# Weight preparation in a streaming trunk: how far ahead weights are begun, where their low parts are added, and what the order planner charges

## The chip, the cores and the metric

The kernel runs on one core of one Trainium2 chip. The metric is device microseconds of one execution. One execution was also taken with the hardware profiler; its records are what the views of the trace show.

## The reference, cut to what matters

One layer of a hybrid encoder is applied to 512 prompt rows and 64 sample rows of width 1024, which the kernel treats as one block of 576 columns, features on the 128 partitions:

```
x += Mixer(RMSNorm(x))         # gated DeltaNet branch and GLA branch, both in chunks, sigmoid-gated merge, output projection
x += CrossAttn(RMSNorm(x))     # 4 heads into 256 memory tokens (keys and values projected here too)
x += ConvFFN(RMSNorm(x))       # up-projection to 2*2816, causal conv of width 3, silu(gate)*value, down-projection
y  = RMSNorm(x)
```

Outputs are y for both groups of rows, the new matrix states and convolution states, and the projected memory keys and values. All data are float32, so the projections need more than one pass of reduced precision.

## The kernel before, in words

**Weights and their two parts.** Every weight tile is 128 x 1024 float32. A DMA from SyncE's queue loads it from HBM into a raw tile (`raw_tile`, ring of RAWB = 3). It is then split into a high part h (the value rounded to the matmul's format) and a low part lo (what the rounding lost), each a tile of a ring of WB = 6 (`w_tile`). Activations are split likewise. A projection of one weight (`proj`) is, for each of eight blocks k of 128 rows, h*a, h*b and lo*a, each in two column groups of 256 and 320: 48 matmuls. With `late=True` the sixteen lo*a matmuls come after all the others. The first two weights are split by hand at the start; `emit_weight` does all the others.

**Two ways to make lo.** For most weights ScalarE casts raw into h, and then VectorE or GpSimd, whichever the planner expects to be done first (`X`), computes raw - h into lo. For the kinds in `SUMMED` (before: only the FFN's "up" and "dn") `split_summed` lets ScalarE write -raw, rounded, into lo, and raw, rounded, into h; then a DMA issued by GpSimd adds raw to lo, so that the remainder is left. Before, that DMA reads the raw tile in SBUF.

**How far ahead.** `weight(kind, idx)` hands the next weight of the fixed list WORDER to TensorE's code and calls `fetch`, which emits weights until the room of five (or two) tiles is used: the current weight and one more. A part of the FFN's down-projection is done by a product scheme (`emit_product`, `products`): for each pair of output tiles seven products P1, Q5, Q6, P2, P3, Q7, Q4 in place of eight, with weights that are sums of quarters, computed by VectorE into slots named ws. A product's weight takes one w tile (h and lo in its halves), a pair holds two raw tiles until its last product has been split.

**Order of the work.** All queues are in order, and the program is written out by a planner in Python, the class `Driver`. Main code (`main`) yields matmuls of the projections; side chains (`c_gdn`, `c_gla`, `c_att`, `c_gate`, `c_act`) are generators that the driver advances between main pieces. For each instruction the driver charges a cost (FIXED and PACE for VectorE V, ScalarE A, GpSimd G and DMA D; `matmul` for TensorE), works out when its operands would be there, and puts it into a heap by that time; a step of a chain is placed on TensorE once its inputs are expected to be ready. So the costs decide the order of every queue, and an expectation that is too early shows as TensorE waiting.

**Memory.** A pool `tp` holds the small tiles of the side chains (about 24 KB per partition); it stays open to the end. A slot ring of 57 tiles holds everything of 576 columns; PSUM has two double-bank tiles (`big`) and four single-bank ones (`sm`).

**Stages on the time axis.** Start to 30 us; head projections with the DeltaNet and GLA chains between them, to about 360 us; the rest of the gate projections, `out` and `wo` to 540; memory keys and values, queries and attention to 690 (the `mo` projection reaches to about 720); the FFN from there, in which stretches of `up` projections alternate with the product scheme (about 810 to 855, 925 to 970, 1035 to 1085, 1130 to 1150); the final norm and stores. Nearly all instructions are recorded under L211, the line at which the driver issues them, so tiles and times tell them apart.

Of the kernel before, what the change touches and what calls it, by code (L numbers as in the profile page):

```python
# [17 lines left out]
P = 128  # L18
# [11 lines left out]
WB = 6  # L30
NGDN = 2
# [89 lines left out]
SUMMED = ("up", "dn")  # L121
# [11 lines left out]
class Engine:  # L133
# [8 lines left out]
    def weigh(self, calls):  # L142
        cost, aps, outs = 0.0, [], []
        for name, args, kw in calls:
            a = [v for v in list(args) + list(kw.values()) if hasattr(v, "tensor")]
            if kw.get("op") == ALU.pow:
# [3 lines left out]
            cost += 0.05 * (name == "activation") + 0.06 * (name == "scalar_tensor_tensor" or self.key == "V" and a[0].shape[-1] <= 128 and any(v.space == bass.MemoryType.PSUM for v in a[1:]))  # L150
            cost += 0.09 * (kw.get("accum_out") is not None or hasattr(kw.get("scale"), "tensor"))
# [4 lines left out]
        return cost, outs, aps  # L156

    def when(self, calls):
        cost, outs, aps = self.weigh(calls)
        return self.drv.place(self.key, self.drv.open(outs, aps), cost, False) + cost  # L160

    def together(self, calls, extra=0.0):

        cost, outs, aps = self.weigh(calls)
        self.drv.note(self.key, cost + extra, outs, aps, [(getattr(self.eng, name), args, kw) for name, args, kw in calls])
# [15 lines left out]
class Driver:  # L181
# [4 lines left out]
    FIXED = dict(V=0.07, A=0.05, G=0.12, D=0.01)  # L186
    PACE = dict(V=1 / 960, A=1 / 1140, G=1 / 470, D=512 / 360e3)

    def __init__(self, pe, sync):
        self.pe, self.sync = pe, sync  # L190
        self.chains = []
        self.done = set()
        self.now = 0.0
        self.half = None
        self.last = 0.0
        self.wrote = {}
        self.seen = {}
        self.ringed = {}
        self.busy = dict(V=[], A=[], G=[], D=[])
        self.ring = {}  # L200
        self.heap = []
        self.count = 0
# [48 lines left out]
    def free_at(self, tag):  # L251
        return min((max([0.0] + list(self.wrote.get(old, {}).values()) + list(self.seen.get(old, {}).values())), old)
                   for old in self.ring[tag])
# [4 lines left out]
    def place(self, key, t, cost, keep=True):  # L258

        q = self.busy[key]  # L260
        t = max(t, self.now - BACK)
        i = 0
        while i < len(q) and q[i][0] < t + cost:
            t = max(t, q[i][1])
            i += 1
        if keep:
            q.insert(i, (t, t + cost))
        if len(q) > 200:
            del q[:100]
        return t  # L270

    def note(self, key, cost, outs, aps, fns):
        start = self.place(key, self.open(outs, aps), cost)
        end = start + cost
        self.mark(self.wrote, end, outs)
        self.mark(self.seen, end, aps)
        self.last = max(self.last, end)
        self.put(start, fns)

    def load(self, out, in_):  # L280
        cost = self.FIXED["D"] + free(out) * self.PACE["D"]
        start = self.place("D", max(self.ready_at(out), self.latest(self.seen, out)) + 1.6, cost)
        self.mark(self.wrote, start + cost, [out])
        self.put(start - 1.6, [(self.sync.dma_start, (out, in_), {})])

    def store(self, out, in_):
        cost = self.FIXED["D"] + free(in_) * self.PACE["D"]
        start = self.place("D", self.ready_at(in_) + 1.6, cost)
        self.mark(self.seen, start + cost, [in_])
        self.put(start - 1.6, [(self.sync.dma_start, (out, in_), {})])  # L290
# [21 lines left out]
    def matmul(self, out, lhsT, rhs, **kw):  # L312
        n, m = free(rhs), lhsT.shape[-1]
        if lhsT.dtype == F32:
            cost = max(n / 2400, 0.053) if m == 32 else max(n * 4 / 2400 + 0.005, 0.213 if m > 64 else 0.11)
# [75 lines left out]
def tile_trunk(ctx, tc, xT, memT, wt, wd, vec, cst, w0, wgate, st_gdn, st_conv, st_gla, st_ffn, ckT, cv,  # L391
# [12 lines left out]
    tp = ctx.enter_context(tc.tile_pool(name="tp", bufs=6))  # L404
    pb = ctx.enter_context(tc.tile_pool(name="pb", bufs=2, space=bass.MemoryType.PSUM))
    pq = ctx.enter_context(tc.tile_pool(name="pq", bufs=4, space=bass.MemoryType.PSUM))
    cnt = [0]

# [28 lines left out]

    def raw_tile():
        return drv.rotate("raw", RAWB, wp.tile([P, 1024], F32, tag="raw", name=nm("wr"), bufs=RAWB))

    def w_tile():
        return drv.rotate("w", WB, wp.tile([P, 1024], F32R, tag="w", name=nm("w"), bufs=WB))

    def emit_weight(i):
# [6 lines left out]
        if kind == "dn":  # L451
            m, p = idx
            n = len(PARTS[p]) * 128
            DMA(raw[:, :n], wd[m, :, PART0[p] * 128:PART0[p] * 128 + n])
        else:
            DMA(raw, wt[WIDX[(kind, idx)]])
        h, lo = w_tile(), w_tile()
        if kind in SUMMED:
            split_summed(h[:, :n], lo[:, :n], raw[:, :n])
# [3 lines left out]
        wready[i] = (h, lo)  # L463
# [8 lines left out]
    def emit_product(pair, prod):  # L472
# [3 lines left out]
        if prod == "P1":  # L476
            r = halves_of[pair] = []
            for i in range(2):
                raw = raw_tile()
                DMA(raw[:, :2 * n], wd[m + i, :, PART0[p] * 128:PART0[p] * 128 + 2 * n])  # L480
                r += [raw[:, 0:n], raw[:, n:2 * n]]
        r = halves_of[pair]
        a11, a12, a21, a22 = r[:4]
# [11 lines left out]
        if prod in ("P1", "P2", "Q4"):  # L495
            split_summed(h, lo, src)
        else:
            A.copy(h, src)
            X.tensor_tensor(lo, src, f(h), op=ALU.subtract)
        return h, lo  # L500

    def weight(kind, idx, ahead=1):
# [29 lines left out]
    for t_ in raws:  # L532
        drv.rotate("raw", RAWB, t_)
# [75 lines left out]
    def tile_proj(kind, idx, xs, box):  # L609
# [3 lines left out]
        yield from proj(ps, wh, wl, xs, late=kind in SUMMED and idx > 0)  # L613
# [238 lines left out]
    def c_gdn(h):  # L852
# [178 lines left out]
        for i in range(4):  # L1031
# [3 lines left out]
            pc = sm()  # L1035
            if S is not None:
                PE.matmul(pc[0:n, 0:128], ks_[i], S, start=True, stop=True)
# [3 lines left out]
            else:  # L1041
                R = vb[:, i, :]
            PE.matmul(pc[0:n, 128:256], Y[:, i, :], R, start=True, stop=True)
# [4 lines left out]
            yield  # L1048
            PE.matmul(pc[:, 384:512], ktok[:, i, :], vg[0:n, :], start=True, stop=True)
# [30 lines left out]
    def c_gla(p):  # L1080
# [10 lines left out]
        def pairs(s):  # L1091

            out, full = [], []
            for i in range(3):
                t_ = slot(s)
                w_ = 512 if i < 2 else 256
                G.memset(t_[:, 0:w_], 0.0)
                v_ = t_[:, 0:w_].rearrange("p (t a b) -> p t a b", a=2, b=128)
# [4 lines left out]
        aqb, _ = pairs("aqb")  # L1103
        kgt, kgt2 = pairs("kgt")
# [89 lines left out]
        for c in range(2):  # L1194
            po = sm()
            for tb in range(2):
# [9 lines left out]
                yield  # L1206
            for j in range(2):
                A.copy(r4(ot[j][:, 256 * c:256 * c + 256]), po.rearrange("p (t j d) -> p t j d", t=2, j=2)[:, :, j, :])
        for j in range(2):
# [90 lines left out]
    def main():  # L1300
        acc = slot("acc")
        xg = []
        for i in range(2):
            wready[i] = (w_tile(), w_tile())
# [50 lines left out]
        for q_ in (q6, q7, acc2):  # L1355
            add(V, acc, q_)
        emit_weight(2)
# [4 lines left out]
        (wh0, wl0), (wh1, wl1) = weight("q", 0, 0), weight("k", 0, 1)  # L1362
# [173 lines left out]
        for m in range(2):  # L1536
            wh, wl = weight("mo", m, 1 - m)
# [14 lines left out]

        drv.spawn(c_rstat("n3", [(acc, 0)], 4, True, 2.0))
# [90 lines left out]
        def products(pairs):  # L1644

            banks = {}
            for pair, prod in product_order(pairs):
# [8 lines left out]
                wh, wl = weight("dn*", (pair, prod))  # L1656
# [10 lines left out]
                fetch(wpos[0], 5)  # L1667
# [16 lines left out]
        for kd, i in FFN[:-1]:  # L1684
# [17 lines left out]
            else:  # L1702
# [3 lines left out]
                for m in i:  # L1706
                    ps = big()
                    wh, wl = weight("dn", (m, 3), m == i[0])
# [218 lines left out]
```

## Time and profile before

| | |
|---|---|
| median of 3 runs | 1170.57 us (1168.15 to 1171.87) |
| the profiled execution's own time | 1171.68 us |
| its span, first to last instruction | 1169.9 us |
| mean granted TensorE clock | 0.99 |
| busy: TensorE matmul / weight load | 1128.3 us / 1081.6 us |
| busy: VectorE / ScalarE / GpSimd | 725.1 / 540.4 / 338.1 us |
| DMA | 131.08 MB moved, HBM read 92.35 MB |

The page lists busy time by engine (PE is TensorE's matmul, PEld its weight load, DVE VectorE, ACT ScalarE, POOL GpSimd, SP SyncE), the chain of work that ended last, and groups of instructions as "out<-in". In names, wr is a raw weight tile, w a split one, wt the weights in HBM, wd the down-projection in HBM, ws a sum of quarters, xh/xl and the like the two parts of an activation, sm and big PSUM tiles. A view of stages gives for each stretch its length, the busy time and number of instructions of each engine, the granted clock as a share of full speed, the busy share of the 16 DMA engines and GB/s. Matmuls overlap, so a busy TensorE may still be slower than its best; the pitch of matmuls in a pure stretch shows the best.

### The profile page before, as it was taken

The numbers are of one execution on the slowest core, as the hardware profiler recorded it, in microseconds if no ns is written. First come the engines' busy times: TensorE is split into PE (matmuls) and PEld (weight loads), VectorE is DVE, ScalarE is ACT, GpSimd is POOL, SyncE is SP. The second block draws the span as 40 slices with busy tenths as digits, with TensorE's granted clock in tenths as the row PEclk, the third lists the DMA queues.
The fourth block names the chain that finished last, engine by engine and source line by source line (L and its number), as shares of the span: only waits on it lengthen the run. The fifth ranks groups of instructions, "written<-read, shape, count | busy, mean of one in ns | idle before, by whom it ended". The sixth has DMA issues, their size and how long they took to land.

```text
span 1169.9 us, 21282 instructions
## 1 busy us (share of the span) xinstructions
PE 1128.3 (96%) x8453; PEld 1081.6 (92%) x8453; DVE 725.1 (62%) x1316; ACT 540.4 (46%) x1050; POOL 338.1 (29%) x520
## 2 busy tenths in 40 slices
PE   7999999999999999999999999999899989999987
PEld 7899889989889999998999999999899979998986
DVE  7798557677454347556564554557746764677475
ACT  5445337345342242234443344655445545564554
POOL 4373137532202020002221102335333322333232
PEclk9999999999999999999999999999999999999998
DMA  6121102111213323433443324766578657665754
GB/s 230 37 87 43 53 8 73 60 38 42 69 46 113 116 75 119 133 109 118 153 123 104 99 82 111 166 152 138 126 187 186 126 121 192 161 148 137 173 107 122
DMA packets 48883, 131.08 MB, mean 112 GB/s; under 512 B 5648, under 2 KB 16400, under 8 KB 48784
## 3 DMA queue, kind: packets, MB, share of 16 engines
q1 hardware_dynamic: 35824, 97.74, 26.5%
q0 software_dynamic: 12960, 31.99, 15.4%
q8 instruction: 67, 1.10, 0.4%
q14 instruction: 32, 0.26, 0.1%
HBM read 92.35 MB, written 5.37 MB: 84 GB/s over the span
## 4 chain that ended last, share of the span: by engine, by line
PE 78%; DVE 10%; DMA 5%; issue 3%; ACT 3%; POOL 0%; SPq 0%; ACTq 0%; DVEq 0%; POOLq 0%
PE big L211 62%; PE sm L211 16%; DVE c L211 3%; DMA w<-wr 3%; DMA wr<-wd 2%; ACT w L211 1%; DVE x L211 1%; DVE w L211 1%; DVE ws L211 1%; DVE acc L211 1%; DMA x<-xT 1%; DVE fc L211 0%; DVE xl L211 0%; SPq L211 0%; ACT c L211 0%
## 5 line engine op out<-in xcount | busy, mean ns | idle before, releaser
L211 PE MATMUL big<-xh,w 128*128 128x256 f32 (+1 forms) x3072 | 563.1, 299 | 3.3 <-DVE sg L211 1.8
L211 PEld LDWEIGHTS big<-xh,w 128*128 128x128 f32 x3072 | 467.7, 189 | 9.0 <-issue 2.6
L211 PE MATMUL big<-xl,w 128*128 128x256 f32 (+1 forms) x1536 | 328.8, 296 | 2.3 <-DVE xl L211 2.2
L211 PEld LDWEIGHTS big<-xl,w 128*128 128x128 f32 x1536 | 258.5, 189 | 3.1 <-DVE xl L211 3.1
L211 ACT CAST w<-wr 128x1024 fp32r<-128x1024 f32 (+3 forms) x184 | 164.6, 897 | 32.1 <-PE big L211 15.2
L211 POOL TENSOR_TENSOR w<-wr,w 128x1024 fp32r<-128x1024 f32 x37 | 92.0, 2486 | 264.2 <-ACT w L211 241.1
L211 PE MATMUL sm<-ach,w 128*128 128x288 f32 (+1 forms) x496 | 108.4, 305 | 13.7 <-DVE x L211 8.5
L211 POOL DMA_DIRECT2D w<-wr x90 | 78.4, 878 | 146.3 <-ACT w L211 126.5
L211 PEld LDWEIGHTS sm<-ach,w 128*128 128x128 f32 x496 | 83.3, 192 | 18.9 <-DVE x L211 6.7
L211 DVE SCALAR_TENSOR_TENSOR fc<-fu,vec,fc 128x578 f32<-128x578 f32 x88 | 75.2, 856 | 26.4 <-ACT fc L211 25.1
L211 DVE TENSOR_TENSOR w<-wr,w 128x1024 fp32r<-128x1024 f32 (+1 forms) x57 | 69.2, 1217 | 23.8 <-ACT w L211 20.1
L211 DVE TENSOR_TENSOR fu<-big,rbc 128x512 f32<-128x512 f32 x88 | 36.1, 452 | 71.3 <-PE big L211 68.0
L211 ACT ACTIVATE w<-wr 128x1024 fp32r<-128x1024 f32 (+3 forms) x90 | 69.9, 776 | 17.8 <-DMA wr<-wt 10.2
L211 PE MATMUL sm<-acl,w 128*128 128x288 f32 (+1 forms) x248 | 69.7, 299 | 0.0
L211 ACT ACTIVATE fc<-fu,vec 128x578 f32<-128x578 f32 x44 | 38.4, 873 | 66.7 <-DVE fu L211 65.1
L211 POOL COPY fout<-fu 128x2 f32<-128x2 f32 x88 | 24.0, 309 | 108.4 <-DVE fu L211 108.4
L211 ACT CAST w<-ws 128x384 fp32r<-128x384 f32 (+1 forms) x56 | 27.6, 496 | 55.5 <-DVE ws L211 37.9
L211 DVE SCALAR_TENSOR_TENSOR c<-u,vec,c 128x579 f32<-128x579 f32 x36 | 49.5, 1381 | 5.0 <-ACT c L211 4.2
L211 DVE TENSOR_TENSOR x<-x,sm 128x288 f32<-128x288 f32 (+1 forms) x100 | 42.8, 444 | 12.3 <-PE sm L211 12.2
L211 PEld LDWEIGHTS sm<-acl,w 128*128 128x128 f32 x248 | 47.5, 192 | 0.0
L211 PE MATMUL big<-aoh,w 128*128 128x256 f32 (+1 forms) x256 | 45.4, 296 | 0.0
L211 PE MATMUL big<-oh,w 128*128 128x256 f32 (+1 forms) x256 | 44.7, 294 | 0.0
(333 smaller groups left out, 1854.0 us busy)
## 6 DMA issues: line engine op xcount, KB each, us to landing
wr<-wt SPq DMA_DIRECT2D x134, 512.0 KB, 3.7
w<-wr POOLq DMA_DIRECT2D x44, 512.0 KB, 5.2
wr<-wd SPq DMA_DIRECT2D x24, 384.0 KB, 3.4
w<-wr POOLq DMA_DIRECT2D x36, 192.0 KB, 4.1
x<-xT SPq DMA_DIRECT2D x16, 288.0 KB, 4.2
wr<-wd SPq DMA_DIRECT2D x8, 256.0 KB, 2.6
o_y<-yo SPq DMA_DIRECT2D x8, 256.0 KB, 3.3
wr<-wt SPq DMA_DIRECT2D x4, 256.0 KB, 5.1
```

The lines of the kernel that those rows point to most:

```text
L211: fn(*args, **kw)
```

## The change

1. **Further ahead.** Tiles that are still to be read are kept in a set (`pending`), from `keep` until `drop`. `fetch` now emits weights until all w tiles are pending: two weights beyond the current one with six tiles. After `mo` everything held is flushed, the pool `tp` is closed and a pool `fp` opened in its place, with WF = 6 more w tiles: twelve in the FFN.
2. **Low parts.** `SUMMED` holds all kinds but the memory's "mk" and "mv"; the product Q5 is made that way too. The adding DMA reads the weight from HBM again (for Q5, the slot ws), so the raw tile is free once ScalarE has read it twice. Projections by `tile_proj` of all these kinds use the late order.
3. **The planner's account.** FIXED, PACE and other costs change; VectorE operations that share GpSimd's memory port, and GpSimd's own, are also booked on a common line "port"; a DMA is expected 2.2 us after its issue in place of 1.6, at 320 GB/s in place of 360.
4. **Chains.** The DeltaNet state step takes a PSUM tile for each of its parts in place of one for all; GLA's memsets yield; a yield in its output loop moves.

```diff
+WF = 6
-SUMMED = ("up", "dn")
+SUMMED = ("q", "k", "v", "za", "zb", "qb", "kb", "vb", "gta", "gtb", "out", "wo", "mq", "mo", "up", "dn")
...
-                cost += self.drv.FIXED[self.key] + max(free(v) for v in a) * self.drv.PACE[self.key]
+                twice = self.key == "V" and len(ins) == 1 and self.port([(name, args, kw)])
+                cost += self.drv.FIXED[self.key] + n * self.drv.PACE[self.key] * (0.5 if twice else 1.0)
...
-    FIXED = dict(V=0.07, A=0.05, G=0.12, D=0.01)
-    PACE = dict(V=1 / 960, A=1 / 1140, G=1 / 470, D=512 / 360e3)
+    FIXED = dict(V=0.15, A=0.17, G=0.2, D=0.01)
+    PACE = dict(V=1 / 960, A=1 / 1180, G=1 / 465, D=512 / 320e3)
...
-    def place(self, key, t, cost, keep=True):
-        q = self.busy[key]
+    def place(self, key, t, cost, keep=True, port=False):
+        qs = [self.busy[key]] + ([self.busy["port"]] if port else [])
...
-        start = self.place("D", max(self.ready_at(out), self.latest(self.seen, out)) + 1.6, cost)
+        start = self.place("D", max(self.ready_at(out), self.latest(self.seen, out)) + 2.2, cost)
...
     def accumulate(self, out, in_, issuer):
-        issue = self.place("G", self.open([out], [in_]), 1.0)
+        issue = self.place("G", self.open([out], []), 1.0)
...
-        self.mark(self.seen, end, [in_])
...
-            cost = max(n / 2400 + 0.0025, 0.109)
+            cost = max(n / 2228 + 0.0027, 0.109)
...
     def w_tile():
-        return drv.rotate("w", WB, wp.tile([P, 1024], F32R, tag="w", name=nm("w"), bufs=WB))
+        if fp is not None and (len(drv.ring.get("wf", ())) < WF or drv.free_at("wf") < drv.free_at("w")):
+            t_ = drv.rotate("wf", WF, fp.tile([P, 1024], F32R, tag="wf", name=nm("w"), bufs=WF))
+        else:
+            t_ = drv.rotate("w", WB, wp.tile([P, 1024], F32R, tag="w", name=nm("w"), bufs=WB))
+        wnames.add(t_[:].tensor.name)
+        return keep(t_)
...
-    def split_summed(h, lo, raw):
+    def split_summed(h, lo, raw, src):
         A.activation(lo, raw, AF.Copy, scale=-1.0)
         A.copy(h, raw)
-        drv.accumulate(lo, raw, nc.gpsimd)
+        drv.accumulate(lo, src, nc.gpsimd)
...
-        if prod in ("P1", "P2", "Q4"):
-            split_summed(h, lo, src)
+        if prod in ("P1", "P2", "Q4", "Q5"):
+            split_summed(h, lo, src, {"P1": d11, "P2": d12, "Q4": d22}.get(prod, src))
...
-    def weight(kind, idx, ahead=1):
+    def weight(kind, idx, ahead=True, held=False):
...
-        if kind != "dn*":
-            fetch(i, 5 if ahead else 2)
+        for j in [j for j in wready if j < i - held]:
+            drop(*wready.pop(j))
+        if i not in wready:
+            emit_weight(i)
+        if ahead:
+            fetch(i + 1)
         return wready[i]
-    def fetch(i, room):
+    def fetch(i):
+        room = WB + (WF if fp is not None else 0)
         for j in range(i, len(WORDER)):
-            room -= 1 if WORDER[j][0] == "dn*" else 2
-            if room < 0:
+            if j in wready:
+                continue
+            if len(drv.pending & wnames) + (1 if WORDER[j][0] == "dn*" else 2) > room:
                 break
-            if j not in wready:
-                emit_weight(j)
+            emit_weight(j)
...
-        yield from proj(ps, wh, wl, xs, late=kind in SUMMED and idx > 0)
+        yield from proj(ps, wh, wl, xs, late=kind in SUMMED)
...
+        drv.flush(float("inf"))
+        tctx.close()
+        nonlocal tp, fp
+        tp = fp = ctx.enter_context(tc.tile_pool(name="fp", bufs=WF))
         drv.spawn(c_rstat("n3", [(acc, 0)], 4, True, 2.0))
```

More of the change, by code (lines that the diff above doesn't have):

```diff
@@ L145, in weigh @@
             a = [v for v in list(args) + list(kw.values()) if hasattr(v, "tensor")]
+            ins = [v for v in a[1:] if free(v) > 1]
+            n = max(free(v) for v in a)
             if kw.get("op") == ALU.pow:
@@ L148, in weigh @@
             else:
-                cost += self.drv.FIXED[self.key] + max(free(v) for v in a) * self.drv.PACE[self.key]
-            cost += 0.05 * (name == "activation") + 0.06 * (name == "scalar_tensor_tensor" or self.key == "V" and a[0].shape[-1] <= 128 and any(v.space == bass.MemoryType.PSUM for v in a[1:]))
-            cost += 0.09 * (kw.get("accum_out") is not None or hasattr(kw.get("scale"), "tensor"))
+                twice = self.key == "V" and len(ins) == 1 and self.port([(name, args, kw)])
+                cost += self.drv.FIXED[self.key] + n * self.drv.PACE[self.key] * (0.5 if twice else 1.0)
+            cost += 0.06 * (name == "scalar_tensor_tensor" or self.key == "V" and a[0].shape[-1] <= 128 and any(v.space == bass.MemoryType.PSUM for v in a[1:]))
+            cost += 0.2 * (kw.get("accum_out") is not None) + 0.09 * hasattr(kw.get("scale"), "tensor")
             outs.append(a[0])
@@ L156, in weigh, with port @@
         return cost, outs, aps
+    def port(self, calls):
+        if self.key != "V":
+            return self.key == "G"
+        for name, args, kw in calls:
+            a = [v for v in list(args) + list(kw.values()) if hasattr(v, "tensor")]
+            here = [v for v in a[1:] if free(v) > 1 and v.space != bass.MemoryType.PSUM]
+            if len(here) > 1 or len(here) == 1 and name in ("tensor_copy", "tensor_scalar") and a[0].space != bass.MemoryType.PSUM:
+                return True
+        return False
     def when(self, calls):
         cost, outs, aps = self.weigh(calls)
-        return self.drv.place(self.key, self.drv.open(outs, aps), cost, False) + cost
+        return self.drv.place(self.key, self.drv.open(outs, aps), cost, False, self.port(calls)) + cost
     def together(self, calls, extra=0.0):
         cost, outs, aps = self.weigh(calls)
-        self.drv.note(self.key, cost + extra, outs, aps, [(getattr(self.eng, name), args, kw) for name, args, kw in calls])
+        self.drv.note(self.key, cost + extra, outs, aps, [(getattr(self.eng, name), args, kw) for name, args, kw in calls], self.port(calls))
 class Either:
@@ L198, in __init__ @@
         self.ringed = {}
-        self.busy = dict(V=[], A=[], G=[], D=[])
+        self.busy = dict(V=[], A=[], G=[], D=[], port=[])
         self.ring = {}
+        self.pending = set()
         self.heap = []
@@ L251, in free_at, with note @@
     def free_at(self, tag):
-        return min((max([0.0] + list(self.wrote.get(old, {}).values()) + list(self.seen.get(old, {}).values())), old)
-                   for old in self.ring[tag])
+        return min((max([0.0] + list(self.wrote.get(old, {}).values()) + list(self.seen.get(old, {}).values()))
+                    if old not in self.pending else float("inf"), old) for old in self.ring[tag])
     def open(self, outs, aps):
         return max(self.ready_at(*aps), self.latest(self.seen, *outs)) + HOP
-    def place(self, key, t, cost, keep=True):
-        q = self.busy[key]
+    def place(self, key, t, cost, keep=True, port=False):
+        qs = [self.busy[key]] + ([self.busy["port"]] if port else [])
         t = max(t, self.now - BACK)
[L262 to L269, printed above, removed]
-        return t
-    def note(self, key, cost, outs, aps, fns):
-        start = self.place(key, self.open(outs, aps), cost)
+        while True:
+            at, before = [], t
+            for q in qs:
+                i = 0
+                while i < len(q) and q[i][0] < t + cost:
+                    t = max(t, q[i][1])
+                    i += 1
+                at.append(i)
+            if t == before or len(qs) == 1:
+                break
+        for q, i in zip(qs, at):
+            if keep:
+                q.insert(i, (t, t + cost))
+            if len(q) > 300:
+                del q[:100]
+        return t
+    def note(self, key, cost, outs, aps, fns, port=False):
+        start = self.place(key, self.open(outs, aps), cost, True, port)
         end = start + cost
@@ L1655, in products @@
                 o = banks[bank][:, 0:HT]
-                wh, wl = weight("dn*", (pair, prod))
+                wh, wl = weight("dn*", (pair, prod), False)
                 for i, ke in enumerate(kes):
```

66 lines of the change are left out of this document (43 added, 23 removed).

## The prediction

> **What bounds the kernel now.** I read the page's totals first, then the view of stages, then who waited for whom in the stages that lose time, then the chain through one of them.
>
> ```profile
> span 1169.9 us, 21282 instructions
> PE 1128.3 (96%) x8453; PEld 1081.6 (92%) x8453; DVE 725.1 (62%) x1316; ACT 540.4 (46%) x1050; POOL 338.1 (29%) x520
> ```
>
> TensorE bounds it: 1169.9 - 1128.3 = 41.6 us of idle is nearly all that a change of order can win, since this change removes no matmul. The stages show where it lies.
>
> ```profile
> core 0: us, PE busy (x) PEld busy (x) DVE busy (x) ACT busy (x) POOL busy (x), PEclk, DMA share, GB/s
> 0.00:30.00 30.00, 23.82 (x156) 20.85 (x156) 21.23 (x23) 15.79 (x25) 14.22 (x20) 0.96 0.64 228
> 30.00:360.00 330.00, 320.96 (x2556) 294.50 (x2549) 227.67 (x449) 149.25 (x428) 129.59 (x169) 0.99 0.17 54
> 360.00:540.00 180.00, 179.20 (x1363) 178.99 (x1362) 95.35 (x148) 58.88 (x84) 13.94 (x13) 1.00 0.34 107
> 540.00:690.00 150.00, 149.25 (x1039) 140.05 (x1040) 86.40 (x155) 63.87 (x127) 27.52 (x12) 1.00 0.36 114
> 810.00:870.00 60.00, 55.36 (x406) 53.77 (x406) 37.12 (x73) 28.30 (x50) 19.28 (x33) 1.00 0.68 153
> 870.00:930.00 60.00, 60.00 (x457) 60.00 (x456) 40.63 (x67) 35.80 (x50) 24.13 (x54) 1.00 0.71 158
> 930.00:990.00 60.00, 54.12 (x396) 52.31 (x395) 35.46 (x75) 27.12 (x48) 16.77 (x30) 1.00 0.69 159
> 1050.00:1090.00 40.00, 37.06 (x260) 35.84 (x259) 24.23 (x52) 16.65 (x32) 11.17 (x17) 0.96 0.69 158
> 1122.00:1150.00 28.00, 21.85 (x141) 19.81 (x140) 22.30 (x46) 17.68 (x37) 11.09 (x14) 0.95 0.52 103
> 1150.00:1170.00 20.00, 14.68 (x105) 14.07 (x103) 8.77 (x22) 6.89 (x13) 2.35 (x4) 0.84 0.35 121
> ```
>
> Length less PE busy: the start loses 6.2 us, the chains' stage 9.0, the two stages from 360 to 690 together 0.8 + 0.75 = 1.6, the four stretches with the product scheme 4.64 + 5.88 + 2.94 + 6.15 = 19.6, the last 20 us 5.3. That is 41.7. An `up` stretch (870 to 930) loses nothing, at a DMA share of 0.71. So these four stretches, 188 us, hold half of the loss. What TensorE waits for there (810 to 1150 us), what VectorE waits for in the same window, and what SyncE's queue waits for over the whole run:
>
> ```profile
> PE sm L211 <- DVE x L211: 8.5, 8, 2.3
> PE sm L211 <- DMA w<-wr: 6.9, 5, 2.0
> PE sm L211 <- ACT w L211: 2.7, 4, 1.1
> DVE ws L211 <- DMA wr<-wd: 19.4, 11, 3.1
> SPq L211 <- DMA w<-wr: 359.8, 72, 10.9
> ```
>
> Read from the bottom: the raw reload waits for the adding DMA that still reads the raw tile (359.8 us); VectorE, in order, then stands 19.4 us in front of a sum of quarters whose raw tile has not landed; the `x` additions that free a PSUM bank are queued behind it (8.5 us of TensorE), and the split weights come late too (6.9 + 2.7). The chain through the first such stretch says the same:
>
> ```profile
> 813.83 4.56 DMA w<-wr
> 818.44 3.03 DMA wr<-wd
> 826.35 3.51 DMA wr<-wd
> 847.01 8.46 DMA w<-wr
> ```
>
> **Part 1: weights begun further ahead, raw tiles freed earlier, twelve w tiles in the FFN.** The best pace, from a pure stretch of the chain (later than the last side chain):
>
> ```profile
> 358.88 77.78 PE big L211 x588
> ```
>
> 77.78 / 588 = 132 ns a matmul, so a weight of 48 takes 6.35 us and a pair's seven products of nine each 8.3 us. Before, a product's weight could be begun five tiles, that is some four products or 5 us, ahead of its use; the chain above shows one reload and one low part in series, 3.0 to 3.5 plus 4.6 to 8.5 us, with ScalarE between them. That does not fit in 5 us. With twelve tiles it is eleven products, 13 us, and the first pair of a stretch is prepared during the last `up` tiles. The reload no longer has the adding DMA ahead of it. What is late next is the raw ring, still three: a pair's second raw tile is free only when the pair before has formed its Q7 sum. But that sum is now paced by w tiles and not by TensorE, and 3.5 us fits in a pair's 8.3.
> So I take three quarters of the 19.6 us out: -14.7. The quarter left stands for the first products after the last activation, which wait for activations and not weights. The granted clock adds something: 0.96 of 40 us and 0.95 of 28 us is 1.6 + 1.4 us of half-speed time behind those idle stretches; I take half, -1.5. Bounds: nothing, and 19.6 + 3.0 = -22.6.
>
> **Part 2: low parts by adding DMAs in all stages.** Removed are subtractions, added are a ScalarE pass, an issue on GpSimd and a DMA for each. Durations, by shape, and from the list of DMA issues:
>
> ```profile
> L211 ACT ACTIVATE w<-wr 128x1024 fp32r<-128x1024 f32 x44 | 46.2, 1050 | 13.5 <-DMA wr<-wt 10.2 <-issue 3.2
> L211 POOL TENSOR_TENSOR w<-wr,w 128x1024 fp32r<-128x1024 f32 x37 | 92.0, 2486 | 264.2 <-ACT w L211 241.1 <-DVE q L211 23.0
> L211 POOL DMA_DIRECT2D w<-wr x90: 849/860/1174, 711.5 to 1147.0; - x90
> wr<-wt SPq DMA_DIRECT2D x134, 512.0 KB, 3.7
> w<-wr POOLq DMA_DIRECT2D x44, 512.0 KB, 5.2
> ```
>
> Where the subtractions are: on GpSimd, then on VectorE, in 30 to 360 and in 360 to 540 us (instructions on tile w alone).
>
> ```profile
> 30.00:360.00 330.00, 56.98 (x23) 0.99 0.17 54
> 360.00:540.00 180.00, 6.05 (x3) 1.00 0.34 107
> 30.00:360.00 330.00, 9.72 (x8) 0.99 0.17 54
> 360.00:540.00 180.00, 31.81 (x26) 1.00 0.34 107
> ```
>
> In 30 to 360: 31 weights. ScalarE gains 31 x 1.05 = 33 us (149 to 182 of 330); GpSimd loses 57 and gains 31 x 0.88 = 27; VectorE loses 9.7. In 360 to 540: 29 weights, ScalarE 59 to 89 of 180, VectorE 95 to 64. No engine comes near TensorE. Queued behind GpSimd's issue, which waits for ScalarE's first pass, is the chains' own GpSimd work; its wait was for a ScalarE cast before as well, and is now followed by 0.86 us and not 2.49.
> The latency grows: a low part was there one ScalarE pass and one subtraction after its tile came free (at most 1.05 + 2.49 = 3.5 us); now it is one pass and one landing, 1.05 + 5.2 = 6.3 us. Against that, a third weight begins at the start of the tile two before it: 12.7 us, and the late order adds 32 x 0.132 = 4.2 (not for `out`). The adding DMA from HBM is not in the trace; the nearest rows are the plain load from HBM, 3.7 us, below, and the longest adding DMA of the chain, 8.46 us, above. I take 5.2, the same operation from SBUF: with 8.46 the low part is there after 9.5 us, still inside 12.7. So no wait, by 3 to 6 us of cover; if the cover were gone, each microsecond over costs 60 weights x 1 us. Only behind the memory weights, whose 24 matmuls are half a tile, is it tight: two of them (6.4 us) plus 4.2 is 10.6 against 6.3 to 9.5.
> GpSimd's issue was 849/860/1174 ns (least, median, most) among 90, beside a VectorE that is busy 36 to 41 of 60 us. The Trainium skill's page "SBUF — State Buffer" (the section on the two separate sides, its box on the "DVE blocks DMA" trap, and the section behind it) says that a GpSimd-issued DMA can be locked out by a two-port VectorE operation, about 620 ns alone against 3100 ns overlapped. No row here shows that in the issue. By the page each added low part would be about 2.5 us later, an estimate: 8.8 us at the median landing, still covered; only the four queries behind memory weights could be late, and the sum would be some 4 us more.
> I take +1.5 us for this part from 360 to 690 us, where almost nothing is lost now and a new wait can only cost. Bounds: -1.6 (all idle there gone) and +10.
>
> **Part 3: the planner's account, and the chains' PSUM tiles.** In 30 to 360 us TensorE's named waits are all for VectorE, in chain steps placed too early:
>
> ```profile
> PE sm L211 <- DVE S L211: 2.2, 2, 1.1
> PE sm L211 <- DVE tg L211: 2.2, 1, 2.2
> PE big L211 <- DVE sg L211: 1.8, 1, 1.8
> ```
>
> The old account charges VectorE 0.07 + 128/960 = 0.20 us for a 128-column step and a matmul of this kernel 288/2400 + 0.0025 = 0.122 us; the pitch is 0.132, and the new account says 0.132. The ScalarE pass is charged 1.04 us by the new account (0.17 + 1024/1180), 0.95 to 1.0 by the old, 1.05 in the row. So the steps of a chain come a little later, mostly after their inputs. The chains have room for this: `out` needs them, and its matmuls start late:
>
> ```profile
> L211 PE MATMUL big<-oh,w x256: 275/304/364, 431.7 to 482.9; 128*128 128x256 f32 x128
> ```
>
> The last chain piece ends before the pure stretch at 358.9, so there are 73 us to spare. I take 4 of the 9.0 us out. But a new order of some 2500 matmuls also makes new misfits: bounds -9 and +9.
>
> **Part 4: start and end.** The first weight after the hand-made two is now split by two ScalarE passes at a time when ScalarE prepares activations (15.8 of 30 us); the end keeps its norm and stores. Nothing, -2 to +2. The flush before the FFN's pool only fixes an order that is a few us deep: inside that bound.
>
> **Sum.** -14.7 - 1.5 + 1.5 - 4 = -18.7 from the profiled execution's own 1171.68 us (its span and 1.8 around it): 1153.0. The median of the runs is 1.1 lower than that execution; I leave the number at 1153. With half of part 1 and a mixer 2 us worse it is 1164, with nearly all of parts 1 and 3 1141: the forecast's own range.
>
> **The rivals.**
> *The stall moves to the raw ring.* Three raw tiles are unchanged, and half of the chain's DMA time above is the reload (3.0 and 3.5 us). If the sums of quarters still wait for reloads, only the directly named 2.7 + a little goes, and the mixer's order gives it back: 1168 to 1171, say 1169. Against it: 359.8 us of the queue's waiting was for the DMA that no longer holds raw.
> *The DMA engines fill (slower).*
>
> ```profile
> q1 hardware_dynamic: 35824, 97.74, 26.5%
> q0 software_dynamic: 12960, 31.99, 15.4%
> ```
>
> Adding DMAs took 15.4% of 1169.9 = 180 us for 31.99 MB, that is 2.95 us of all engines for a 0.52 MB weight. In 360 to 540 us 29 more of them bring the share from 0.34 to 0.34 + 29 x 2.95/180 = 0.82; TensorE lost nothing at 0.71. If reading HBM makes them dearer by a factor over (1 - 0.34)/0.475 = 1.39, this stage is bound by DMA. At 1.6 it is 1.10, 18 us longer, and the `up` stretches, where such DMAs hold 2.95/6.35 = 0.46 of the 0.71, reach 0.99, so that the gain of part 1 shrinks to some 5: 1185. For it: HBM is read twice. Against: plain loads move 97.74 MB in 310 us of engine time, 315 GB/s, so the source is not what makes adding slow.
> *More is gained.* PE's busy time overlaps and hides slow pitches. By weight loads (PEld) the chains' stage idles 330 - 294.5 = 35.5 us, not 9. If the better account takes a third of that, -12 in place of -4, and part 1 its whole 22.6: 1138. The page "Trainium Kernel Development and Optimization" of the Trainium skill (Performance Expectations) says that matmul busy time is a bad measure of what is left and weight-load busy share a good one; that favours this case. Against it: the small float32 matmuls there load rarely for their length, and no named wait accounts for the difference.
>
> **How the numbers follow.** Forecast 0.58, raw ring 0.15, DMA full 0.15, more 0.12. About 0.3%, 3.5 us, is what a measurement of this kernel can tell from no change. Faster: 0.58 + 0.12 + 0.03 of the raw ring's case = 0.73; same 0.10, the most of that case; slower 0.17, with 0.02 for an order that is worse by more than part 1 gives. The range 1136 to 1178 leaves out most of the DMA case and half of the last: 0.18.
>
> **What would show it.** Right: the four stretches' idle falls from 19.6 to about 5 us, VectorE's wait for reloads (19.4) nearly vanishes, the queue's wait for the adding DMA is gone, 360 to 690 stays within 2 us of idle at a DMA share near 0.8 in its first part. Wrong: waits of TensorE for w tiles' DMAs between 360 and 690; idle of the chains' stage above 9 us; an adding DMA over 9 us from issue to landing; reload waits that stay.

## The result, and the profile after

The changed kernel takes 1142.01 us (median of 4, 1141.34 to 1142.56) against 1171.22 us (median of 4 runs of the kernel before beside it); the ratio is 0.9753, 95% interval 0.9729 to 0.9776. The prediction, 1153.0 with a range of 1136 to 1178, had the direction and some three fifths of the size. The profiled execution took 1141.34 us, 30.3 less than the one before.

The totals, the waits of SyncE's queue and the DMA queues after:

```profile
span 1139.5 us, 21399 instructions
PE 1117.0 (98%) x8453; PEld 1076.4 (94%) x8453; DVE 628.7 (55%) x1296; ACT 618.3 (54%) x1138; POOL 294.8 (26%) x540
```

```profile
SPq L227 <- ACT w L227: 441.3, 99, 20.3
```

```profile
q0 software_dynamic: 25632, 73.41, 37.8%
q1 hardware_dynamic: 35824, 97.74, 26.2%
```

TensorE's idle falls from 41.6 to 22.5 us, its busy time by another 11.3, with the same 8453 matmuls. Most of the 11.3 is the clock. The trace's records of the granted clock hold six intervals of 3.41 us at 0.50, half speed, under matmuls of the kernel before (from 27.4, 51.3, 65.0, 1065.1, 1147.0 and 1160.6 us), and one of the changed kernel (from 725.8). Half of the busy time in them is lost: 10.1 us before, 1.7 after. One of them with the time around it, in the kernel before:

```profile
1061.70:1065.10 3.40, 1.19 (x8) 0.94 (x8) 1.71 (x4) 0.93 (x2) 0.69 (x1) 1.00 0.94 183
1065.10:1068.50 3.40, 3.40 (x17) 3.40 (x16) 3.11 (x9) 1.26 (x3) 0.00 (x0) 0.50 0.39 117
1068.50:1071.90 3.40, 3.40 (x27) 3.40 (x27) 2.11 (x5) 2.36 (x6) 2.09 (x3) 1.00 0.42 47
```

First TensorE idles for 2.2 us, then it does 17 matmuls at half clock where the next stretch has 27. Six of the seven intervals have 1.6 to 2.4 us of idle in the 3.4 us ahead of them (the one at 1160.6 has 0.65). So in these two traces a stall can cost up to 1.7 us beyond its length. Other stalls as long (1.98 us at 961.8, 2.35 at 1131.6, both before) have no such interval behind them, and that a stall causes it is not shown. Where the other 3 us of the 11.3 come from stays open.

The reload of a raw tile no longer waits for an adding DMA (359.8 us before) but for ScalarE's pass. ScalarE is busy 78 us longer, nearly all of it the first passes for 74 more whole weights (118 adding DMAs of 512 KB against 44) at 1.05 us each.

The stages of the prediction, after:

```profile
core 0: us, PE busy (x) PEld busy (x) DVE busy (x) ACT busy (x) POOL busy (x), PEclk, DMA share, GB/s
0.00:30.00 30.00, 26.12 (x176) 24.02 (x177) 19.95 (x27) 19.61 (x29) 14.34 (x25) 1.00 0.81 258
30.00:360.00 330.00, 328.29 (x2628) 302.09 (x2627) 194.54 (x435) 181.83 (x460) 92.12 (x169) 1.00 0.49 107
360.00:540.00 180.00, 179.96 (x1328) 177.13 (x1327) 69.85 (x139) 86.48 (x115) 30.35 (x39) 1.00 0.76 185
540.00:690.00 150.00, 149.87 (x1088) 144.26 (x1087) 71.37 (x149) 78.18 (x143) 11.51 (x14) 1.00 0.63 164
690.00:810.00 120.00, 115.69 (x859) 114.82 (x858) 68.91 (x133) 68.35 (x98) 36.84 (x83) 0.99 0.68 153
```

Since the stages move, fixed stretches no longer hold the same work. So the time is told below by landmarks: the start of the first matmul of `out`, `wo` and the memory keys, of the first `up`, and the first and last matmul of each product stretch (252, 252, 252 and 96 matmuls in every kernel). Each is read from one profiled execution. Four of the kernels below run the changed kernel's program unaltered up to the FFN, and there `out` starts at 419.1, 419.2, 419.3 and 419.8, so a difference under 1 us at that point says nothing.

| from one landmark to the next, us | before | after | difference |
|---|---|---|---|
| start to `out` (head projections, chains, gates) | 431.7 | 419.1 | -12.6 |
| `out`, `wo` | 102.2 | 102.8 | +0.6 |
| memory, attention, `mo` | 186.7 | 183.7 | -3.0 |
| first `up` to first product | 90.8 | 96.7 | +5.9 |
| product stretches | 39.3, 41.3, 39.5, 24.6 | 34.7, 34.7, 34.8, 19.3 | -21.2 |
| `up` stretches between them | 76.6, 76.1, 45.7 | 76.4, 76.4, 45.8 | +0.2 |
| end | 15.5 | 15.3 | -0.2 |

The product stretches by busy time, first the kernel before, then the changed one, cut at those landmarks:

```profile
811.40:850.80 39.40, 35.02 (x254) 33.67 (x253) 28.26 (x58) 19.62 (x39) 13.45 (x19) 1.00 0.63 136
927.30:968.60 41.30, 35.42 (x254) 33.61 (x252) 28.09 (x62) 19.29 (x38) 11.80 (x15) 1.00 0.62 137
1044.70:1084.20 39.50, 36.56 (x254) 35.14 (x253) 28.78 (x62) 19.78 (x40) 11.83 (x15) 0.96 0.62 142
1129.80:1154.40 24.60, 19.17 (x121) 17.59 (x120) 18.14 (x41) 16.13 (x33) 7.46 (x8) 0.93 0.40 76
```

```profile
802.30:837.00 34.70, 33.76 (x253) 33.28 (x253) 23.86 (x52) 20.88 (x37) 13.42 (x19) 1.00 0.85 195
913.30:948.00 34.70, 33.77 (x253) 33.31 (x253) 23.87 (x52) 21.14 (x37) 13.22 (x19) 1.00 0.86 188
1024.30:1059.10 34.80, 33.87 (x254) 33.41 (x253) 24.53 (x53) 21.55 (x37) 12.31 (x18) 1.00 0.86 188
1104.90:1124.20 19.30, 16.67 (x121) 16.00 (x121) 13.91 (x31) 13.83 (x27) 6.53 (x7) 1.00 0.45 76
```

Idle falls from 18.6 to 5.4 us, busy time from 126.2 to 118.1 for the same matmuls. Of those 8.1 us, 3.2 are the two half-clock intervals (clock 0.96 and 0.93), which are gone.

One stage is worse. What TensorE waited for, and the timeline around it (ScalarE's and VectorE's instructions; in brackets the idle time before and its cause):

```profile
PE big L227 <- DMA wr<-wt: 3.9, 1, 3.9
```

```profile
714.79 1.06 ACT L227 ACTIVATE w<-wr 128x1024 fp32r<-128x1024 f32 x1 [1.18 <-DMA wr<-wt]
...
720.92 1.06 ACT L227 ACTIVATE w<-wr 128x1024 fp32r<-128x1024 f32 x1 [4.13 <-DMA wr<-wt]
721.88 1.03 ACT L227 CAST w<-wr 128x1024 fp32r<-128x1024 f32 x1
...
722.82 0.69 ACT L227 COPY rbc<-sm 128x512 f32<-128x512 f32 x2
723.43 1.55 DVE L227 TENSOR_TENSOR fu<-big,rbc 128x512 f32<-128x512 f32 x4 [8.33 <-ACT rbc L227]
```

As the FFN's pool opens, room for three more weights comes at once. Their splits stand in ScalarE's queue ahead of its copy of the norm statistics (`rbc`); the last of them waits 4.1 us for its raw tile, the copy with it, then VectorE's evacuation of the `up` tiles, and so TensorE for a PSUM tile. The wait's name, a DMA, is only its far end. Behind it comes the changed kernel's one half-clock interval: 3.9 + 1.7 us is nearly all of the 5.9.

### The profile page after: what moved, and what is told of

Its sections match the earlier page's. It is cut to its first block, busy times and chain, and to the rows that moved or that the text cites. A ratio compares the mean times of both kernels' runs of the same rounds, so it can differ in the third digit from the quotient of the medians.

```text
span 1139.5 us, 21399 instructions
## 1 busy us (share of the span) xinstructions
PE 1117.0 (98%) x8453; PEld 1076.4 (94%) x8453; DVE 628.7 (55%) x1296; ACT 618.3 (54%) x1138; POOL 294.8 (26%) x540
## 3 DMA queue, kind: packets, MB, share of 16 engines
q0 software_dynamic: 25632, 73.41, 37.8%
## 4 chain that ended last, share of the span: by engine, by line
PE 93%; DVE 3%; ACT 2%; DMA 1%; issue 0%; SPq 0%; POOL 0%; ACTq 0%
PE big L227 70%; PE sm L227 22%; DMA wr<-wt 1%; ACT w L227 1%; DVE x L227 1%; DVE fc L227 0%; DVE c L227 0%; SPq L227 0%; ACT xh L227 0%; DVE acl L227 0%; ACT sq L227 0%; DVE xl L227 0%; DVE gy L227 0%; DVE w L227 0%; DVE gna L227 0%
## 5 line engine op out<-in xcount | busy, mean ns | idle before, releaser
L227 PE MATMUL big<-xh,w 128*128 128x256 f32 (+1 forms) x3072 | 554.8, 300 | 6.7 <-DMA wr<-wt 3.9
L227 POOL DMA_DIRECT2D w<-wt x118 | 103.3, 882 | 445.4 <-ACT w L227 411.9
L227 ACT ACTIVATE w<-wr 128x1024 fp32r<-128x1024 f32 (+3 forms) x164 | 148.6, 906 | 109.8 <-PE big L227 52.9
L227 PE MATMUL sm<-ach,w 128*128 128x288 f32 (+1 forms) x496 | 103.4, 297 | 5.4 <-DVE x L227 5.4
L227 POOL COPY fout<-fu 128x2 f32<-128x2 f32 x88 | 34.9, 427 | 123.4 <-DVE fu L227 123.2
L227 POOL DMA_DIRECT2D w<-wd x46 | 40.9, 915 | 69.0 <-ACT w L227 68.9
L227 PE MATMUL big<-mgh,w 128*128 128x256 f32 (+1 forms) x256 | 44.6, 295 | 0.0
L227 PEld LDWEIGHTS big<-oh,w 128*128 128x128 f32 x256 | 38.5, 188 | 0.3 <-DMA w<-wt 0.3
L227 PEld LDWEIGHTS big<-mgh,w 128*128 128x128 f32 x256 | 38.7, 189 | 0.0
```

What stands on the lines that cost most here:

```text
L227: fn(*args, **kw)
```

## The experiments

Theory 1 was the prediction's: distance wins the product stretches, the account wins the stage before `out`. Theory 2, taken from the two traces, gives the latter to GpSimd's relief from subtractions, which had held VectorE up. It rests on this row of the kernel before and that of the changed one (30 to 360 us):

```profile
L211 DVE SCALAR_TENSOR_TENSOR c<-u,vec,c 128x579 f32<-128x579 f32 x36 | 49.5, 1381 | 5.0 <-ACT c L211 4.2
```

```profile
L227 DVE SCALAR_TENSOR_TENSOR c<-u,vec,c 128x579 f32<-128x579 f32 x36 | 29.5, 822 | 2.3 <-ACT c L227 1.5
```

**The old account in the changed kernel.**

```diff
-    FIXED = dict(V=0.15, A=0.17, G=0.2, D=0.01)
-    PACE = dict(V=1 / 960, A=1 / 1180, G=1 / 465, D=512 / 320e3)
+    FIXED = dict(V=0.07, A=0.05, G=0.12, D=0.01)
+    PACE = dict(V=1 / 960, A=1 / 1140, G=1 / 470, D=512 / 360e3)
...
+        qs = [self.busy[key]]
...
+            cost = max(n / 2400 + 0.0025, 0.109)
```

> The changed kernel with the planner's old costs (FIXED, PACE, matmul, 1.6 us to a DMA, no common port). The changed kernel reaches the first matmul of out 12.6 us earlier than the kernel before (419.1 against 431.7). Theory 1 (better placed steps won that): that point moves back by 8 to 12 us, and TensorE's named waits for VectorE in 30 to 360 us return to about 9; total 1150 to 1156. Theory 2 (GpSimd's long subtractions had held VectorE up, and their removal won it): that point stays within 3 us of 419, total 1142 to 1147.

Measured: 1137.32 us, ratio 0.9716 (0.9702 to 0.9731). `out` starts at 421.4, only 2.3 later, of which 1.7 are one half-clock interval (from 72.1 us); first `up` to first product takes 92.1 in place of 96.7; product stretches 34.2, 34.2, 34.1. Theory 1 fails on the account: the new one is worth about 2 us in the chains' stage, and with the other edits the old one is the faster by 4.7 us in all, which neither theory expected.

**Subtractions again outside the FFN.**

```diff
+SUMMED = ("up", "dn")
```

> The changed kernel with low parts outside the FFN made by subtraction again, as before; everything else stays. Theory 1 (account): out starts within 3 us of 419.1, total 1140 to 1145. Theory 2 (GpSimd's subtractions hold VectorE): VectorE's convolution step of 579 columns goes from 822 ns back towards 1381, out starts 8 to 12 us later, total 1150 to 1155.

Measured: 1148.68 us, 0.9812 (0.9797 to 0.9826); `out` at 426.6, 7.5 later. This edit takes away the adding DMAs and, since `late` hangs on the same list, the late order; together they carry 7.5 of the 12.6, and 3.4 of the 7.5 are two half-clock intervals (from 36.6 and 217.6 us). But the mechanism that theory 2 named is not it:

```profile
L227 DVE TENSOR_TENSOR w<-wr,w 128x1024 fp32r<-128x1024 f32 x30 | 36.5, 1219 | 1.0 <-PE big L227 0.7
L227 DVE SCALAR_TENSOR_TENSOR c<-u,vec,c 128x579 f32<-128x579 f32 x36 | 29.2, 819 | 2.1 <-ACT c L227 1.4
```

The planner, charging for the common port, gave 30 of the subtractions to VectorE; the convolution step is as short as after the change (819 ns, against 1381 before), and `out` is late all the same.

**Subtractions, with the late order of the low part.**

```diff
+SUMMED = ("up", "dn")
+LATE = ("q", "k", "v", "za", "zb", "qb", "kb", "vb", "gta", "gtb", "out", "wo", "mq", "mo", "up", "dn")
...
-        yield from proj(ps, wh, wl, xs, late=kind in SUMMED)
+        yield from proj(ps, wh, wl, xs, late=kind in LATE)
```

> The changed kernel with low parts outside the FFN made by subtraction, but the late order of the low part's matmuls kept for all kinds. Subtraction with the old order put out at 426.6 in place of 419.1. If the late order carries those 7.5 us: out at 419 to 422, total 1141 to 1145. If VectorE's 36 us of subtractions carry them: out at 425 to 428, total 1147 to 1150.

Measured: 1145.61 us, 0.9778 (0.9762 to 0.9794); `out` at 423.1. Between the two expectations: of the 7.5 us about half (3.5) is the order, in which by the prediction's estimate the low part is wanted 4 us later, the rest (4.0) the subtractions. VectorE's 29.5 us of them in 30 to 360 us are the likely part, which is not shown. The split is rough: this run has one half-clock interval ahead of `out`, the run before had two.

**Six w tiles in the FFN.**

```diff
-        room = WB + (WF if fp is not None else 0)
+        room = WB
...
-        if fp is not None and (len(drv.ring.get("wf", ())) < WF or drv.free_at("wf") < drv.free_at("w")):
+        if False:
```

> The changed kernel with six w tiles in the FFN too (no tile is taken from the new pool). Theory 1 (distance won the product stretches): they go from 34.7 us back to 38 to 41 each, +15 in all, while the 4 us wait at the start of the FFN goes; total about 1152. Rival (the raw tiles freed by reading HBM won them): stretches stay below 36 us, total 1136 to 1144.

Measured: 1160.78 us, 0.9922 (0.9906 to 0.9939). That is 9 over the expectation. Product stretches 40.3, 43.3, 39.3 and 24.4: all of the gain there is gone, and 2.6 us more. The start of the FFN is back at 91.1. TensorE's first waits:

```profile
PE sm L227 <- DMA w<-ws: 12.6, 9, 2.1
PE sm L227 <- DVE x L227: 5.8, 8, 1.4
PE sm L227 <- DMA w<-wd: 2.6, 2, 2.2
```

The worst is the low part of Q5, which the change made an adding DMA: dear without distance, free with it.

**The adding DMA from the raw tile in SBUF, which it holds.**

```diff
-        drv.accumulate(lo, src, nc.gpsimd)
+        drv.accumulate(lo, raw, nc.gpsimd)
...
+        self.mark(self.seen, end, [in_])
```

> The changed kernel with the adding DMA reading the raw tile in SBUF, which is held until it has landed. If freeing raw early is what counts: reloads wait for the adding DMA again, the product stretches go from 34.7 to 37 us or more and stages of 6.35 us a weight begin to lose, total 1150 to 1165. If distance alone counts: stretches stay at 35, total 1140 to 1145. Landing of the adding DMA falls from 7.2 to about 5.2 us if HBM is what made it longer, and stays near 7 if the fuller DMA engines did.

Measured: 1145.05 us, 0.9785 (0.977 to 0.98). `out` at 418.1, product stretches 35.1, 34.6, 34.8, 19.3; only the start of the FFN is longer, 100.3: ScalarE waits 8.3 us there for a raw tile, in place of 4.1, and 6.8 us at half clock begin in TensorE's stall. So freeing raw tiles early is not what won. Landings, in the list of DMA issues, of the changed kernel and then of this one:

```profile
wr<-wt SPq DMA_DIRECT2D x134, 512.0 KB, 5.7
w<-wt POOLq DMA_DIRECT2D x118, 512.0 KB, 7.2
```

```profile
wr<-wt SPq DMA_DIRECT2D x134, 512.0 KB, 4.4
w<-wr POOLq DMA_DIRECT2D x118, 512.0 KB, 5.4
```

**HBM as the source, in the kernel before.**

```diff
-        drv.accumulate(lo, raw, nc.gpsimd)
+        drv.accumulate(lo, src, nc.gpsimd)
...
-        self.mark(self.seen, end, [in_])
```

> The kernel before with the FFN's adding DMAs reading HBM, so that raw tiles are free earlier; nothing else. If reloads held by the adding DMA were the cause of the waits in the product stretches: stretches of 39 to 41 us fall to 36 to 37, VectorE's wait for reloads from 19.4 to under 8, total about 1160. If the distance of five tiles is what binds: stretches fall by 1 us or less, total 1167 to 1171.

Measured: 1179.59 us, 1.0055 (1.0036 to 1.0074): slower by half a per cent. Product stretches 43.9, 41.3, 40.9, 24.6. VectorE's wait for reloads grows from 19.4 to 27.0 us, and the reload lands later. First VectorE's wait and the landings in this run, then the reload in the kernel before:

```profile
DVE ws L211 <- DMA wr<-wd: 27.0, 10, 4.1
w<-wt POOLq DMA_DIRECT2D x44, 512.0 KB, 7.1
wr<-wd SPq DMA_DIRECT2D x24, 384.0 KB, 5.3
```

```profile
wr<-wd SPq DMA_DIRECT2D x24, 384.0 KB, 3.4
```

**Distance alone.** The changed kernel's `pending`, `fetch` and pool, with the old account, kinds, source and chains.

```diff
+        room = WB + (WF if fp is not None else 0)
         for j in range(i, len(WORDER)):
-            room -= 1 if WORDER[j][0] == "dn*" else 2
-            if room < 0:
+            if len(drv.pending & wnames) + (1 if WORDER[j][0] == "dn*" else 2) > room:
                 break
```

> Distance alone: old account, old kinds of low parts (adding DMAs from the raw tile in SBUF, in the FFN only), old chains, but weights emitted until all w tiles are pending, and twelve tiles in the FFN. If distance alone won the product stretches, as the runs with six tiles and with raw as the source suggest: stretches of 34 to 35.5 us, the one at the end 19 to 20, out at 428 to 432 as before, total 1150 to 1155. If it needs the raw tiles to be free early as well: stretches of 36 us or more, total over 1157.

Measured: 1159.78 us, 0.9899 (0.9882 to 0.9915). The product stretches:

```profile
818.00:853.50 35.50, 34.08 (x253) 33.39 (x253) 23.52 (x51) 18.79 (x33) 11.00 (x18) 1.00 0.73 154
930.10:965.10 35.00, 34.16 (x253) 33.45 (x252) 23.52 (x51) 18.21 (x33) 10.33 (x14) 1.00 0.74 158
1041.60:1076.80 35.20, 34.14 (x253) 33.44 (x252) 23.79 (x50) 18.86 (x33) 13.10 (x19) 1.00 0.77 170
1122.70:1142.10 19.40, 16.47 (x122) 16.03 (x121) 14.18 (x32) 14.26 (x28) 5.05 (x6) 1.00 0.41 76
```

Distance by itself wins 19.6 of the 21.2 us there and 2.8 of the 3.0 in the attention stage; `out` starts at 429.0, 2.7 earlier. The total, 5 over the expectation, misses because of the burst: from first `up` to first product 101.9 us, 11 more than before (ScalarE waits 8.0 us for a raw tile, and 10.2 us at half clock begin in TensorE's stall).

**The new account alone, in the kernel before** (the diff of the first experiment, the other way).

> The kernel before with the new account alone. Theory 1 (account won the stage before out): out starts at 419 to 424 in place of 431.7, total 1158 to 1164, with the product stretches still at 39 to 41 us, or a few us less since reloads are expected later. Theory 2 (GpSimd's relief won it): out starts at 428 or later, total 1166 to 1172; since the common port is booked, some subtractions may go to VectorE, and its convolution step then falls below 1381 ns.

Measured: 1188.47 us, 1.0133 (1.0117 to 1.0149): slower, where both theories had it no slower than before. `out` starts at 439.1, though the convolution step is down to 820 ns, which speaks against theory 2's mechanism once more.

```profile
PE sm L225 <- DVE x L225: 16.6, 23, 2.7
PE big L225 <- DVE w L225: 16.4, 6, 7.2
```

The account moved subtractions to VectorE (77 of the 90 whole weights in place of 53), a weight was begun only one ahead, and TensorE waits for low parts, up to 7.2 us at a time.

**The chains' old PSUM tile and yields.**

```diff
+            pc = sm()
             if S is not None:
-                pc = sm()
                 PE.matmul(pc[0:n, 0:128], ks_[i], S, start=True, stop=True)
...
-            pc = sm()
             PE.matmul(pc[0:n, 128:256], Y[:, i, :], R, start=True, stop=True)
...
```

> The changed kernel with the DeltaNet state step in one PSUM tile again, GLA's memsets without a yield and the yield of its output loop where it was. If the separate PSUM tiles carry part of the 12.6 us won before out: out starts 3 to 8 us later than 419.1, total 1145 to 1150. If not: within 2 us, total 1140 to 1144.

Measured: 1145.59 us, 0.9768 (0.9753 to 0.9782), an interval that overlaps the changed kernel's. `out` at 421.1, 2.0 later; the start of the FFN 98.6, 1.9 longer, which has nothing to do with these chains except through the order. At most 2 us, and not settled.

**Room for six until the norm statistics are used.**

```diff
-        room = WB + (WF if fp is not None else 0)
+        room = WB + (WF if fp is not None and drv.ready("ffn") else 0)
...
                     use_norm("n3")
+                    drv.done.add("ffn")
```

> The changed kernel with the room for weights held at six tiles until the FFN's norm statistics have been used, then twelve. In the changed kernel ScalarE's copy of the statistics stands behind a split whose raw tile lands late, TensorE waits 3.9 us at 720 us, and from the first up matmul to the first product takes 96.75 us against 90.79 before. Theory (the burst of splits at the pool's opening blocks ScalarE): the wait goes and that distance falls to 91 to 92; total 1136 to 1138. Rival (the flush before the pool fixes the order badly, whatever is fetched): the wait stays, total 1141 to 1143.

Measured: 1138.59 us, 0.971 (0.9695 to 0.9724), half a microsecond over the expectation. From first `up` to first product 91.1; the first product stretch gives 1.9 us back (36.6). So 5.6 of the 5.9 us come from the burst, and not from the flush, which is the same here. It takes the new account as well: with the old one and the same burst this stretch took 92.1.

**This, with the old account throughout** (the diff above and that of the first experiment together).

> The changed kernel with the old account and the room held at six until the FFN's statistics have been used. If the burst at the pool's opening costs the old account its last 1 to 2 us there: from the first up to the first product 91 us in place of 92.1, total 1135 to 1137. If the late start of the prefetch costs the first product stretch as much: 1137 to 1139.

Measured: 1134.51 us (1134.07 to 1135.76), 0.9684 (0.9667 to 0.97), the fastest median here and ahead of both kernels. First `up` to first product 90.8, product stretches 34.1, 34.2, 34.1, 19.4, `out` at 420.7.

**This, with the new account up to the FFN and the old one from there.**

```diff
         tctx.close()
+        drv.old, drv.LAG = True, 1.6
+        drv.FIXED = dict(V=0.07, A=0.05, G=0.12, D=0.01)
+        drv.PACE = dict(V=1 / 960, A=1 / 1140, G=1 / 470, D=512 / 360e3)
```

> The changed kernel with the new account up to the FFN's pool and the old one from there, and the room held at six until the statistics have been used. If the stages add up: out at 419 to 420, stretches of 34.2, up stretches of 76.1, total 1133 to 1136, the fastest here. If the planner's stages do not add up (a step from one account to the other leaves a misfit): 1137 to 1141.

Measured: 1135.72 us, 0.9698 (0.9681 to 0.9715), not to be told from the one above: `out` at 419.3, but the last product stretch 20.9, with one half-clock interval in it (from 1101.6 us).

## Why the prediction was right or wrong, point by point

The total is inside the range, but not because the terms were right. The stages of parts 1 to 3 won 5.0, 3.9 and 8.6 us more than the sum gave them, and the start of the FFN lost 5.9 that it did not have. That the errors left the total only 11 us off is luck in part. The measured 1142 lies nearer to the rival *more is gained* (1138) than to the forecast (1153).

- **Part 1, right in mechanism, mis-sized.** The forecast took 14.7 us of idle and 1.5 of half-speed time from the product stretches; they gave 21.2. Idle alone fell by 13.2; the rest, 8.1 us, came out of busy time, where the sum had only the 1.5. Of the 8.1, 3.2 are the clock: the prediction's 1.6 + 1.4 us are what the half clock costs (the time at half clock is twice that), and all of it went and not half. Distance was the cause (six tiles: all of it back; distance alone: 19.6). But the prediction's reading of the waits put the raw tiles, held by adding DMAs, at their root; that falls with the runs: freed early without distance the stretches grow, held with distance (two runs) they stay at 35 us. What looked like a held tile was a weight begun too late.
- **The raw-ring rival** did not come: VectorE's 19.4 us wait for reloads is gone from the changed kernel's list of waits on ws, with three raw tiles still.
- **Part 2, the sign was wrong.** The sum had +1.5 us for adding DMAs from 360 to 690 us, as a risk in stages that lose nothing. The low parts did arrive in time: `out` and `wo` cost 0.6 more, at a DMA share of 0.76 against the 0.82 worked out, and the attention stage 3.0 less, 2.8 of it by distance. Not in the sum was what the removed subtractions and the late order were worth in the stage before `out`: 7.5 of the 12.6 us.
- **The DMA rival** did not come: adding DMAs took 37.8% of 1139.5 = 431 us for 73.41 MB, 3.08 us a weight against 2.95, a factor of 1.04 where 1.39 was needed. Their landing did grow, 5.2 to 7.2 us; by the runs with the two sources, 1.8 of that is HBM (7.2 against 5.4), inside the 8.46 that was the bound.
- **The rule on GpSimd-issued DMAs.** Issues took 849/862/1219 ns (least, median, most) among the 118 whole weights, and at most 1566 among the smaller ones. So nothing of the 2.5 us lock-out that the prediction estimated from the page "SBUF — State Buffer" of the Trainium skill shows in the issue. That page of the Trainium skill ties the lock-out to a two-port operation of VectorE. Whether one ran beside an issue is not shown.
- **Why the convolution step was long.** Before, 13 of the 36 steps took over 1 us, and each of these overlaps a two-input operation of GpSimd, 11 of them a subtraction of 2.3 to 3.0 us. The other statement of that page of the Trainium skill, in the section on the two separate sides, that the pair of ports shared by VectorE and GpSimd is locked for a whole instruction, agrees with that. The run with subtractions has the short step and a late `out`, so the step did not make the 7.5 us; whether it is part of the other 5.1 is open. The least, median and longest step in ns, before and after:

```profile
L211 DVE SCALAR_TENSOR_TENSOR c<-u,vec,c x36: 809/822/3023, 42.9 to 250.9; 128x579 f32<-128x579 f32 x36
L227 DVE SCALAR_TENSOR_TENSOR c<-u,vec,c x36: 814/822/865, 39.7 to 236.1; 128x579 f32<-128x579 f32 x36
```

- **Part 3, failed.** The sum gave 4 us to the account. Alone it costs 16 us; in the changed kernel it wins about 2 before `out` and loses 4.6 at the start of the FFN and 1.6 in the product stretches. The stage's gain of 12.6 was three times the 4 mainly for another reason (7.5 us, part 2), with about 2 each from account and perhaps chains, and distance (2.7 alone). The single undoings need not add up. Three half-clock intervals ahead of `out`, 5.1 us in all, are gone too and lie inside these figures; the sum counted the clock in the product stretches alone.
- **Part 4, failed.** The sum gave the FFN's start nothing, and the pool's opening was held inside 2 us; it cost 5.9, through the prefetch in the new account's order and not through the flush.
- **More is gained**, the rival that read weight loads, had the sizes nearly right (12 and 22.6 us, against 12.6 and 21.2) but the wrong cause for the first, the account. Matmul busy time hid 11.3 of the 30.3 us, weight-load busy time only 5.2: idle by weight loads fell from 88.3 to 63.1 us, 25.2 of the 30.3, idle by matmuls by 19.1. The rule of the Trainium skill's page "Trainium Kernel Development and Optimization" (Performance Expectations), that matmul busy time is a bad measure and weight-load busy share a good one, agrees with that. How much of the 63.1 us could still be won no run shows.

## What to carry to other kernels

When a tuned in-order kernel loses time in short stretches, first ask how many steps ahead their inputs are begun; what the waits name may be a symptom of starting late. Room that opens at once is filled at once: put a prefetch burst behind whatever small work shares its queues, here the copy of the norm statistics. A cost model nearer to the rows does not by itself give a better order; run it alone before keeping it. And read the clock's records beside the idle time: here about 8 of the 30 us came back as clock and not as idle.

## What the runs showed of the hardware that was not expected

An adding DMA of 0.52 MB with HBM as its source lands in 7.2 us, in 5.4 us with SBUF as its source, in kernels that are otherwise alike; the engines' time for it differs less, 37.8% of 1139.5 us against 35.7% of 1142.5 for the same 73.41 MB.

```profile
q0 software_dynamic: 25632, 73.41, 35.7%
```

A stall of VectorE behind GpSimd hits single instructions: the convolution step takes 822 ns at the median before and after, but up to 3023 ns before, beside GpSimd's subtractions, and 865 at most after. And a few stalls of TensorE cost more than their length, by half-clock intervals that take 10.1 us of busy time before and 1.7 after.
